# Expert-choice routing in a two-layer backbone: elementwise steps moved from GpSimd to VectorE, and the first expert's weight blocks split during the output projection

## The chip, the cores and the metric

The kernel runs on one core of a Trainium2 chip. A core has five engines, each with its own in-order instruction stream: TensorE (PE; its weight loads are shown as PEld), VectorE (DVE), ScalarE (ACT), GpSimd (POOL) and SyncE (SP), which here issues most of the DMA transfers. They wait for each other by semaphores. The metric is the device time of one execution in microseconds (us), the median of the runs.

## The reference, cut to what matters

One inference step of a backbone with two layers over 1024 latent tokens and 128 prompt tokens of width 1024. Layer 0 mixes the tokens with a recurrent unit (RG-LRU), layer 1 with a spatial gating unit (SGU); each is followed by an expert-choice mixture of experts (MoE) with 16 experts.

```python
def _ec_moe(x, router, w_gate, w_up, w_down):
    cap = EC_FACTOR * (bsz * t) // N_EXPERTS            # 128 of the 1024 tokens, 16 of the 128
    aff = jax.nn.softmax(xf @ router, axis=-1)
    g, idx = lax.top_k(aff.T, cap)                      # every expert chooses its tokens
    xs = xf[idx]
    hh = jax.nn.silu(einsum('ecd,edf->ecf', xs, w_gate)) * einsum('ecd,edf->ecf', xs, w_up)
    out = einsum('ecf,efd->ecd', hh, w_down) * g[..., None]
    y = jnp.zeros_like(xf).at[idx.reshape(-1)].add(out.reshape(-1, d))
...
for l in range(DEPTH):
    y = mixer(hn)                                       # ends with the output projection "@ w_out"
    x = x + g1 * y
    hn = _rmsnorm(x, norm2_g[l]) * (1 + s2) + sh2
    x = x + g2 * _ec_moe(hn, ...)
```

## The kernel before

The tokens are worked on in nine chunks of 128: chunks 0 to 7 are the latent tokens, chunk 8 is the prompt. Weights come from memory in fp32 and are split into two f16 parts, so that each fp32 product becomes three f16 matmuls (high by high, high by low, low by high): ScalarE rounds a block to its upper half (line L1583 in the expert loop, `whi`), VectorE subtracts that from the block for its lower half (L1589, `wlo`). A block has 128 columns of a 1024 by 1024 matrix. An expert has three such matrices, 24 blocks.

**Output projection.** The mixer's output is multiplied by `w_out` chunk by chunk, the last part of `lru_mixer` and `sgu_mixer`. Behind each chunk its residual and norm are computed (class `Post`: `residual`, `turn`, `logits`, `gather`), which gives the router's logits of that chunk. `turn` transposes the normalized rows on PE (hT, L350), `logits_mul` is L361, `gather_mul` L374 (`pz`). Inputs of the next chunks are fetched on SP's queue. The last chunk, 8, overlaps the routing.

**Routing** (class `Route`). The softmax over the experts ends at L386. Then the 128th largest affinity of each expert is found by bisection over its bits in 15 rounds (`rounds`). A round is a chain through two engines: VectorE forms three candidates (L425) and a mask of affinities over them (L427), PE counts by eight small matmuls with ones (L433), VectorE evaluates the counts (L434) and takes the largest (L435), and the next round starts from that. `finish` (from L444) compares with the found threshold and derives the slots of the tokens. The remaining work of chunk 8 is put between these steps by hand: `within[r]` (D in `lead`) holds functions that run between round r's mask and its counts, `after[r]` (R) those that run after its evaluation. `lead` places them relative to round v, which is 5 in layer 0 and 3 in layer 1: `take` multiplies y by the gate and adds it to x (on POOL, L315 and L316; in layer 0 for two halves of 512 columns, in layer 1 for one), then `squares`, `var`, `norm`, `turn(8)`, `halve` (chunk 8's rows as a rounded copy `xph` on ScalarE, L533, and the rest `xpl` on POOL, L534), the logits, the prompt's weights and their spreading.

**Start of the experts' weights.** Raw weights come in loads of 2 MB (L1574), each half a matrix, that is four blocks, into five buffers (`raw`). The five first loads are issued ahead of round 3. With `AHEAD = 3` the first three pairs of blocks are split before the expert loop begins: as many as fit (`route.v + r < 13`) during the rounds by `split_first` (two ScalarE passes, then the subtraction on POOL, L1602), the others after them.

**Expert loop** (`for n in range(NPAIR)`). An expert is twelve groups n of 48 matmuls (L1698) on two blocks: groups 0 to 3 with `w_gate`, 4 to 7 with `w_up`, 8 to 11 with `w_down`. The first 36 matmuls of a group take the first six of eight row slices of both blocks, the last 12 the other two. Groups 0 to 7 read the expert's tokens (`Sh`, `Sl`). Groups 4 to 7 give hidden blocks: t (VectorE, L1714), Hh (ScalarE, L1719, for the last one VectorE, L1721), Hl (VectorE, L1722). Groups 8 to 11 read these. Between the groups' matmuls the later blocks are split, in an order that the tables HIS and LOS give as counts for three places of a group (`ahead(n, 0)` and `ahead(n, 1)` between the group's two parts, `ahead(n, 2)` behind it). `whi` and `wlo` are rings of 12 buffers. At the end of layer 1 the final norm runs in the last expert's groups (class `Final`; its gains on POOL are L1816).

Of the kernel before, what the change touches and what calls it, by code (L numbers as in the profile page):

```python
# [43 lines left out]
def tile_trunk(  # L44
# [186 lines left out]
    def rows(ch):  # L231
        return slice(ch * P, (ch + 1) * P)
# [10 lines left out]
    class Post:  # L243
# [59 lines left out]
        def last(self, yps):  # L303


            l, xt, t = self.l, state["x8"], self.xnp
            g1 = self.g1 if self.apart else gate_row(l, 0, self.pool)
            ss = sm.tile([P, 2], F32, tag="ss2", name=f"pss{l}_8")
            s1, r, v, rr = (sm.tile([P, 1], F32, tag="last", name=f"last{l}_{i}", bufs=4) for i in range(4))
            cs = slice(0, 512), slice(512, 1024)  # L310

            def take():
                for n in sorted(yps):
                    A.activation(t[:, cs[n]], yps[n], AF.Copy, scale=1.0 / (UP * DOWN))
                    G.tensor_tensor(t[:, cs[n]], t[:, cs[n]], g1 if self.apart else g1[:, cs[n]], op=OP.mult)  # L315
                    G.tensor_tensor(xt[:, cs[n]], xt[:, cs[n]], t[:, cs[n]], op=OP.add)  # L316

            def squares():
                for n in sorted(yps):
                    A.activation(t[:, cs[n]], xt[:, cs[n]], AF.Square, accum_out=ss[:, n:n + 1])  # L320

            def var():
                V.tensor_add(s1, self.ss0[:, 8:9] if self.apart else ss[:, 0:1], ss[:, 1:2])
                V.tensor_scalar(v, s1, 1.0 / D, EPS, op0=OP.mult, op1=OP.add)
                G.tensor_tensor(r, v, half, op=OP.pow)

# [7 lines left out]
            return take, squares, var, norm  # L334

# [40 lines left out]
        def gather_keep(self, ch):  # L376
            V.tensor_copy(self.lg[:, ch], self.pz)

    def softmax(l, lg, af, ex):
# [9 lines left out]
    class Route:  # L389
# [93 lines left out]
        def inform(self, part):  # L483

            info, afs, t0 = self.info, self.af[:, 0:8], self.t0
            if part == 0:
                V.tensor_copy(info[:, :, :, 2], afs)
                V.tensor_copy(info[:, :, :, 0:2], tok_c[:, :, None, :].to_broadcast([P, 8, NE, 2]))
                V.tensor_tensor(t0, afs, info[:, :, :, 2], op=OP.subtract)
            else:  # L490
                V.tensor_copy(info[:, :, :, 3], t0)
                V.tensor_tensor(t0, t0, info[:, :, :, 3], op=OP.subtract)
                V.tensor_copy(info[:, :, :, 4], t0)

# [35 lines left out]
        def halve(self):  # L530
            xnp = self.post.xnp.rearrange("t (k p) -> t k p", p=P)
            self.xh, self.xl = (self.room(n, [P, KD, P], F32R) for n in ("xph", "xpl"))
            A.copy(self.xh, xnp)  # L533
            G.tensor_tensor(self.xl, xnp, self.xh, op=OP.subtract)  # L534

# [52 lines left out]
        def lead(self, y8, yps):  # L588


            post = self.post
            take, squares, var, norm = post.last(yps)
            for f in y8[:7]:
# [14 lines left out]
            v = self.v = s + 3  # L608
            R[s].append(take)
            R[v - 1].append(squares)  # L610
            D[v].append(var)
            D[v + 1].append(norm)
            R[v + 2].append(lambda: post.turn(8))
            D[v + 3].append(lambda: self.inform(0))
            R[v + 3].append(self.halve)
            D[v + 4].append(lambda: self.inform(1))
            R[v + 4].append(lambda: post.logits_mul(8))
            D[v + 5].append(lambda: post.logits_keep(8))
            R[v + 5].append(lambda: post.gather_mul(8))
            D[v + 6] += [lambda: post.gather_keep(8), self.weigh]  # L620
            D[v + 7].append(self.share)
            for q in range(4):
                R[v + 7 + q // 2].append(lambda q=q: self.spread(q))
# [6 lines left out]
    def lru_mixer(carry_of):  # L630
# [444 lines left out]
        def split_hg(ch):  # L1075
            hh = tmp("ae", f"hgh{ch}", 2, F16)[:, 0:9 * P].rearrange("p (h t) -> p h t", t=P)
            hl = tmp("hs", f"hgo{ch}", 2, F16)[:, 0:9 * P].rearrange("p (h t) -> p h t", t=P)
            split_up(hgs[ch], hh, hl, DOWN)
            return hh, hl
# [45 lines left out]
        def y_of(ch):  # L1125
            return [ps3.tile([P, 512], F32, tag="y", name=f"y0_{ch}_{n}", bufs=4) for n in range(2)]

        post.fetch(0)
        for ch in range(8):
            hl = nxt  # L1130
# [14 lines left out]
            else:  # L1145
# [14 lines left out]
                post.gather(ch - 1)  # L1160
            post.residual(ch, 1, yps[1])
        hl = nxt
        yps = y_of(8)
# [4 lines left out]
        route.settle(pool_of(ew, "l0x", side="right"))  # L1168
        return post, route, ew.close


    def sgu_mixer(carry_of):
# [72 lines left out]
        def fetch(ch):  # L1245
            if ch < 8:
                xs[ch] = kp.tile([P, D], F32, tag="pr", name=f"x1_{ch}", bufs=4)
                SP.dma_start(xs[ch], x_d[rows(ch), :])

        def norm(*chs):  # L1250
# [7 lines left out]
            for i, ch in enumerate(chs):  # L1258
                x = xs[ch]
                if ch == 8:  # L1260
                    xs[ch] = kp.tile([P, D], F32, tag="pr", name="x1_8", bufs=4)
                V.tensor_scalar_mul(xs[ch], x, r[:, i:i + 1])
# [49 lines left out]
        def load_spatial():  # L1312
            ws = state["ws"] = kp.tile([P, SGG, P], F32, tag="pr", name="ws", bufs=4)
            SP.dma_start(ws, sg_w_s[0].rearrange("g p q -> p g q"))
            SP.dma_start(bsr, sg_b_s[0])
# [173 lines left out]

        post = Post(1, pb, ps1, carry, alloc, apart=True)  # L1490
        post.xt[8] = state["x8"][:, 0:512]
        post.fetch_half(0)
        y, gates = {(0, 0): yps}, {}
        for c in range(1, 68):
# [22 lines left out]
            elif n == 0:  # L1517
# [30 lines left out]
        route.settle(pool_of(ew, "l1x", side="right"))  # L1548
        return post, route, ew.close


    def moe(l, post, route, carry, close):
        es = ExitStack()
# [12 lines left out]

        def load(m, eng=SP):

            if m >= 6 * NE or m == 5 and eng is SP:
# [4 lines left out]
            eng.dma_start(t, w[l, e].rearrange("(k p) f -> p k f", p=P)[:, :, 512 * half:512 * (half + 1)])  # L1574

# [4 lines left out]
        def split_hi(n, b):  # L1580
            if n < NPAIR:
                hi = wp.tile([P, KD, P], F16, tag="whi", name=f"whi{l}_{n}_{b}", bufs=12)
                A.activation(hi, block(n, b), AF.Copy, scale=UP)  # L1583
                ws[n, b] = [hi]

        def split_lo(n, b):
            if n < NPAIR:
                lo = wp.tile([P, KD, P], F16, tag="wlo", name=f"wlo{l}_{n}_{b}", bufs=12)
# [6 lines left out]
        def split_first(n, b):  # L1595

            up = mp.tile([P, KD, 144], F32, tag=("xg", "tmp")[b], name=f"wup{l}_{n}_{b}")[:, :, 0:P]
            A.activation(up, block(n, b), AF.Copy, scale=UP)
            hi = wp.tile([P, KD, P], F16, tag="whi", name=f"whi{l}_{n}_{b}", bufs=12)
            A.copy(hi, up)  # L1600
            lo = wp.tile([P, KD, P], F16, tag="wlo", name=f"wlo{l}_{n}_{b}", bufs=12)
            G.tensor_tensor(lo, up, hi, op=OP.subtract)  # L1602
            ws[n, b] = [hi, lo]
            if n % 2 == 1 and b == 1:
                raws.pop(n // 2)
                load(n // 2 + 5)

# [78 lines left out]


# [243 lines left out]
    for l, mixer in enumerate((lru_mixer, sgu_mixer)):  # L1931
# [6 lines left out]

        post, route, close = mixer(carry_of)
        moe(l, post, route, pools[l], close)  # L1940
        ec.close()
# [57 lines left out]
```

## Time and profile before

| | us |
|---|---|
| median of 3 runs | 2603.92 (2603.43 to 2604.54) |
| profiled execution, in all | 2600.83 |
| its span, first to last instruction | 2599.0 |
| busy: PE 94%, DVE 74%, ACT 63%, POOL 11% of the span | 2431.4, 1914.7, 1640.6, 293.2 |
| memory traffic over the span | 248 GB/s |

The profile is of one execution. Its times are in us from the start of the span, unless ns is written. A line such as L425 is a line of the kernel as printed above. In the timeline, a row is a start, a duration, the engine, line and operation, the tile written and the tile read with shapes and types, how many instructions the row joins (x8), and in brackets how long the engine had been idle before it and what released it. [...] The output projection of layer 0 lies in 400 to 520, its routing in 525 to 566, its expert loop from 581; in layer 1 the projection's second half lies in 1781 to 1889, the routing in 1888 to 1927, the expert loop from 1941.

### The profile page before, as it was taken

The numbers are of one execution on the slowest core, as the hardware profiler recorded it, in microseconds if no ns is written. First come the engines' busy times: TensorE is split into PE (matmuls) and PEld (weight loads), VectorE is DVE, ScalarE is ACT, GpSimd is POOL, SyncE is SP. The second block draws the span as 40 slices with busy tenths as digits, with TensorE's granted clock in tenths as the row PEclk, the third lists the DMA queues.
The fourth block names the chain that finished last, engine by engine and source line by source line (L and its number), as shares of the span: only waits on it lengthen the run. The fifth ranks groups of instructions, "written<-read, shape, count | busy, mean of one in ns | idle before, by whom it ended". The sixth has DMA issues, their size and how long they took to land. (4 is left out here: it accounts for less than half of the span.)

```text
span 2599.0 us, 60553 instructions
## 1 busy us (share of the span) xinstructions
PE 2431.4 (94%) x26054; PEld 1850.1 (71%) x26054; DVE 1914.7 (74%) x2771; ACT 1640.6 (63%) x2348; POOL 293.2 (11%) x324
## 2 busy tenths in 40 slices
PE   6999989959999999997999999999959999999995
PEld 4555554439999999997434455534549999999995
DVE  6888895479999989996622233445689999999997
ACT  5877883347877877785623333433357877777874
POOL 1011101120000000001201100100120000000003
PEclk9999999969999999998999999999969999999998
DMA  9466215359999999995544533455649999999994
GB/s 316 169 205 205 76 63 163 131 197 343 347 351 359 347 337 356 353 348 162 180 151 165 174 114 110 153 189 191 205 182 347 344 357 361 343 334 360 343 358 173
DMA packets 317755, 647.19 MB, mean 249 GB/s; under 512 B 15362, under 2 KB 52790, under 8 KB 317486
## 3 DMA queue, kind: packets, MB, share of 16 engines
q1 hardware_dynamic: 291792, 564.30, 61.0%
q0 software_dynamic: 21136, 74.67, 9.0%
q10 hardware_dynamic: 4558, 4.35, 0.5%
q8 instruction: 204, 3.34, 0.5%
q14 instruction: 65, 0.53, 0.1%
HBM read 576.59 MB, written 66.68 MB: 248 GB/s over the span
## 5 line engine op out<-in xcount | busy, mean ns | idle before, releaser
L1698 PEld LDWEIGHTS <-whi 128*128 128x128 f16 x12288 | 989.1, 98 | 30.6 <-issue 24.2
L1589 DVE SCALAR_TENSOR_TENSOR wlo<-raw,whi 128x1024 f16<-128x1024 f32 x759 | 894.3, 1219 | 20.7 <-ACT whi L1583 20.7
L1698 PE MATMUL mm<-Sh,whi 128*128 128x144 f16 x4096 | 774.8, 227 | 3.8 <-ACT tmp L1644 1.7
L1698 PE MATMUL mm<-Sl,whi 128*128 128x144 f16 x4096 | 774.7, 226 | 0.9 <-DVE Sl L1656 0.9
L1698 PE MATMUL mm<-Sh,wlo 128*128 128x144 f16 x4096 | 774.7, 227 | 0.0
L1583 ACT ACTIVATE whi<-raw 128x1024 f16<-128x1024 f32 x759 | 755.2, 1060 | 0.0
L1698 PEld LDWEIGHTS <-wlo 128*128 128x128 f16 x6144 | 602.4, 98 | 14.0 <-issue 14.0
L1698 PE MATMUL mm<-Hh,whi 128*128 128x144 f16 x2048 | 388.7, 226 | 19.0 <-DVE Hh L1721 14.8
L1698 PE MATMUL mm<-Hl,whi 128*128 128x144 f16 x2048 | 387.6, 226 | 8.6 <-DVE Hl L1722 8.6
L1698 PE MATMUL mm<-Hh,wlo 128*128 128x144 f16 x2048 | 387.6, 226 | 0.0
L1290 PE MATMUL uv<-sgw,h_hi 128*128 128x512 f16 x576 | 219.4, 381 | 0.0
L1291 PE MATMUL uv<-sgw,h_hi 128*128 128x512 f16 x576 | 219.3, 381 | 0.0
L1292 PE MATMUL uv<-sgw,h_lo 128*128 128x512 f16 x576 | 219.1, 380 | 0.0
L1296 ACT ACTIVATE uvo<-uv 128x512 f32<-128x512 f32 x72 | 42.9, 596 | 198.7 <-PE uv L1292 198.7
L1742 POOL DMA_INDIRECT x_d<-o,idx x31 | 58.0, 1870 | 959.6 <-ACT o L1741 897.7
L864 PE MATMUL pj<-hn_hi,wh 128*128 128x386 f16 x480 | 158.2, 330 | 1.9 <-ACT hn_hi L116 1.9
L865 PE MATMUL pj<-hn_lo,wh 128*128 128x386 f16 x480 | 157.8, 329 | 0.1
L866 PE MATMUL pj<-hn_hi,wl 128*128 128x386 f16 x480 | 157.9, 329 | 0.0
L1403 DVE SCALAR_TENSOR_TENSOR uvo<-sv,bs,uvo 128x256 f32<-128x256 f32 x72 | 31.5, 479 | 139.9 <-PE sv L1400 139.9
L1309 DVE TENSOR_TENSOR uvo<-uvo,gain 128x512 f32<-128x512 f32 x36 | 24.9, 691 | 133.8 <-ACT uv L1308 133.8
L1644 ACT ACTIVATE tmp<-xgT,modc,ns 128x128 f32<-128x128 f32 x248 | 90.2, 468 | 47.5 <-PE xgT L1631 38.8
L1709 ACT ACTIVATE sg<-mm 128x288 f32<-128x288 f32 x128 | 52.3, 409 | 94.5 <-PE mm L1698 94.3
(402 smaller groups left out, 3807.0 us busy)
## 6 DMA issues: line engine op xcount, KB each, us to landing
raw<-in_moe_w_gate_dram SPq DMA_DIRECT2D x64, 2048.0 KB
raw<-in_moe_w_up_dram SPq DMA_DIRECT2D x64, 2048.0 KB
raw<-in_moe_w_down_dram SPq DMA_DIRECT2D x62, 2048.0 KB
wm<-in_w_mod_dram SPq DMA_DIRECT2D x96, 512.0 KB
m<-mt_d SPq DMA_DIRECT2D x72, 256.0 KB
sgr<-in_sg_w_in_dram SPq DMA_DIRECT2D x32, 512.0 KB
win<-in_lru_w_in_dram SPq DMA_DIRECT2D x20, 512.0 KB
v_d<-uvo POOLq DMA_DIRECT2D x36, 256.0 KB, 2.5
```

The costliest lines, as they stand in the source:

```text
L864: PE.matmul(ps[:, i, 0:WP], wh[:, k], hi[k][:, cs], start=(k == 0), stop=False)
L865: PE.matmul(ps[:, i, 0:WP], wh[:, k], lo[k][:, cs], start=False, stop=False)
L866: PE.matmul(ps[:, i, 0:WP], wl[:, k], hi[k][:, cs], start=False, stop=(k == KD - 1))
L1290: PE.matmul(ps, hi[:, k, cs], th[:, k % 4], start=(k == 0), stop=False)
L1291: PE.matmul(ps, hi[:, k, cs], tl[:, k % 4], start=False, stop=False)
L1292: PE.matmul(ps, lo[:, k, cs], th[:, k % 4], start=False, stop=(k == KD - 1))
L1583: A.activation(hi, block(n, b), AF.Copy, scale=UP)
L1589: V.scalar_tensor_tensor(lo, block(n, b), UP, ws[n, b][0], op0=OP.mult, op1=OP.subtract)
L1644: A.activation(o, ps[h][:, k - 4 * h], AF.Identity, bias=sh2[:, 1, k:k + 1], scale=s2[:, 1, k:k + 1])
L1698: PE.matmul(ps[:, b, 0:144], w[:, k], x[:, k], start=(k == 0 and i == 0), stop=(k == KD - 1 and i == 2))
L1709: A.activation(sg[e][:, js], ps, AF.Silu, scale=1.0 / UP)
L1742: G.indirect_dma_start(out=x_d[0:NS, :], out_offset=bass.IndirectOffsetOnAxis(ap=idxs[:, e:e + 1], axis=0), in_=o, in_offset=None, compute ...
```

## The change

- `take` becomes `gate(n)` and `add(n)`, one VectorE instruction each on 512 columns, placed in `within`: half 1 in rounds v - 2 and v - 1, half 0, which only layer 0 has, in rounds 0 and 1.
- `inform` (VectorE, the affinities in three bf16 parts) is cut in four parts in four rounds.
- `halve` keeps the ScalarE copy; the subtraction goes to VectorE in two halves, `halve_rest(0)` in round v + 4 and `halve_rest(1)` in round v + 8.
- `split_first` and the load on ScalarE's queue are gone. A new class `First` loads the first eight blocks of expert 0's `w_gate` one by one (512 KB, SP's queue) and splits them on ScalarE and VectorE, one behind each of the chunks 0 to 7 of the output projection. The buffers for these loads are ones of the mixer. The rings `whi` and `wlo` keep 12 buffers and move to the pool that lives through both stages. `AHEAD` is 4, the 2 MB loads begin with number 2.
- In layer 0 `split_hg` takes one buffer for both halves; in layer 1 tiles tagged `pr` move to another pool.

```diff
@@ class Post, last
-            def take():
-                for n in sorted(yps):
-                    A.activation(t[:, cs[n]], yps[n], AF.Copy, scale=1.0 / (UP * DOWN))
-                    G.tensor_tensor(t[:, cs[n]], t[:, cs[n]], g1 if self.apart else g1[:, cs[n]], op=OP.mult)
-                    G.tensor_tensor(xt[:, cs[n]], xt[:, cs[n]], t[:, cs[n]], op=OP.add)
+            def gate(n):
+                V.scalar_tensor_tensor(t[:, cs[n]], yps[n], 1.0 / (UP * DOWN), g1 if self.apart else g1[:, cs[n]],
+                                       op0=OP.mult, op1=OP.mult)
+            def add(n):
+                V.tensor_add(xt[:, cs[n]], xt[:, cs[n]], t[:, cs[n]])
...
+    class First:
+        N = 8
+        def __init__(self, l, carry, room):
+            self.l, self.carry, self.room, self.raw, self.parts = l, carry, room, {}, []
+            self.src = moe_w_gate[l, 0].rearrange("(k p) f -> p k f", p=P)
+        def load(self, c):
+            if c < self.N:
+                self.raw[c] = self.room(f"first{self.l}_{c}").rearrange("p (k n) -> p k n", k=KD)
+                SP.dma_start(self.raw[c], self.src[:, :, rows(c)])
+        def split(self, c):
+            if c < self.N:
+                p = [self.carry.tile([P, KD, P], F16, tag=f"w{s}", name=f"w{s}{self.l}_f{c}", bufs=12) for s in ("hi", "lo")]
+                split_up(self.raw.pop(c), *p)
+                self.parts.append(p)
...
@@ class Route
         def halve(self):
-            xnp = self.post.xnp.rearrange("t (k p) -> t k p", p=P)
             self.xh, self.xl = (self.room(n, [P, KD, P], F32R) for n in ("xph", "xpl"))
-            A.copy(self.xh, xnp)
-            G.tensor_tensor(self.xl, xnp, self.xh, op=OP.subtract)
+            A.copy(self.xh, self.post.xnp.rearrange("t (k p) -> t k p", p=P))
+
+        def halve_rest(self, h):
+            ks = slice(4 * h, 4 * h + 4)
+            V.tensor_sub(self.xl[:, ks], self.post.xnp.rearrange("t (k p) -> t k p", p=P)[:, ks], self.xh[:, ks])
...
@@ lead
-            R[s].append(take)
+            for n in sorted(yps):
+                r = v - 2 if n else 0
+                D[r].append(lambda n=n: gate(n))
+                D[r + 1].append(lambda n=n: add(n))
+            D[v - 3].append(lambda: self.inform(0))
             R[v - 1].append(squares)
-            D[v].append(var)
+            D[v] += [var, lambda: self.inform(1)]
             D[v + 1].append(norm)
             R[v + 2].append(lambda: post.turn(8))
-            D[v + 3].append(lambda: self.inform(0))
+            D[v + 2].append(lambda: self.inform(2))
+            D[v + 3].append(lambda: self.inform(3))
             R[v + 3].append(self.halve)
-            D[v + 4].append(lambda: self.inform(1))
+            D[v + 4].append(lambda: self.halve_rest(0))
...
+            D[v + 8].append(lambda: self.halve_rest(1))
...
@@ lru_mixer, output projection
+        firsts = First(0, carry, lambda name: tmp("hs", name, 2)[:, 0:D])
         post.fetch(0)
+        for i in range(2):
+            firsts.load(i)
         for ch in range(8):
...
             post.residual(ch, 1, yps[1])
+            firsts.split(ch)
+            firsts.load(ch + 2)
...
@@ sgu_mixer, output projection
+        firsts = First(1, carry, lambda name: wp.tile([P, D], F32, tag="wr", name=name, bufs=4))
...
                 if ch == 8 and q == 3:
                     post.fetch(0)
+                    for i in range(3):
+                        firsts.load(i)
             else:
+                if q == 3:
+                    firsts.split(ch)
+                    firsts.load(ch + 3)
...
@@ moe
-                hi = wp.tile([P, KD, P], F16, tag="whi", name=f"whi{l}_{n}_{b}", bufs=12)
+                hi = carry.tile([P, KD, P], F16, tag="whi", name=f"whi{l}_{n}_{b}", bufs=12)
...
-        for m in range(5):
+        AHEAD = 4
+        for c, p in enumerate(firsts.parts):
+            ws[divmod(c, 2)] = p
+        for m in range(2, 7):
             load(m)
-        AHEAD = 3
-        first = [(n, b) for n in range(AHEAD) for b in range(2)]
-        for r in (1, 3, 4, 6, 9, 10):
-            if route.v + r < 13:
-                route.after[route.v + r].append(lambda nb=first.pop(0): split_first(*nb))
...
-        load(5, A)
...
-        for n, b in first:
-            split_hi(n, b)
-            split_lo(n, b)
         split_hi(AHEAD, 0)
```

## Rows read from the trace of the kernel before

**Rows 1.** Windows view: stretch, length, busy PE PEld DVE ACT POOL (instructions), PEclk, DMA, GB/s.
```profile
475.00:500.00 25.00, 25.00 (x153) 12.61 (x152) 9.56 (x20) 10.07 (x24) 2.22 (x4) 1.00 0.39 129
...
540.00:560.00 20.00, 6.99 (x84) 5.84 (x84) 17.72 (x44) 13.19 (x20) 8.74 (x4) 0.50 0.67 261
...
707.29:746.10 38.81, 38.27 (x603) 37.95 (x601) 35.66 (x49) 30.73 (x44) 3.20 (x2) 1.00 0.99 353
...
1880.00:1900.00 20.00, 11.58 (x108) 6.44 (x107) 14.44 (x45) 6.29 (x12) 4.18 (x6) 0.80 1.01 377
```

**Rows 2.** VectorE's timeline, routing of layer 0: start us, us, instruction, [idle <-releaser].
```profile
524.86 1.39 DVE L386 TENSOR_TENSOR af<-ex,mx 128x128 f32<-128x128 f32 x1
...
560.17 2.08 DVE L425 TENSOR_TENSOR cand<-cand,bits 128x48 int32<-128x48 int32 x1
...
566.03 0.29 DVE L444 TENSOR_TENSOR ge<-af,cand 128x128 bf16<-128x128 f32 x1
```

**Rows 3.** GpSimd's timeline, same stretch.
```profile
560.06 2.12 POOL L1602 TENSOR_TENSOR wlo<-wup,whi 128x1024 f16<-128x1024 f32 x1 [5.76 <-ACT whi L1600]
```

**Rows 4.** VectorE's timeline, routing of layer 1.
```profile
1887.78 0.29 DVE L386 TENSOR_TENSOR af<-ex,mx 128x128 f32<-128x128 f32 x1
...
1888.18 0.21 DVE L425 TENSOR_TENSOR cand<-cand,bits 128x48 int32<-128x48 int32 x1
...
1889.43 0.21 DVE L434 SCALAR_TENSOR_TENSOR cand<-cnt,cand 128x48 f32<-128x48 f32 x1 [0.45 <-PE cnt L433]
...
1889.96 0.21 DVE L425 TENSOR_TENSOR cand<-cand,bits 128x48 int32<-128x48 int32 x1
...
1927.27 0.29 DVE L444 TENSOR_TENSOR ge<-af,cand 128x128 bf16<-128x128 f32 x1
```

**Rows 5.** VectorE's and ScalarE's timelines, rounds 7 and 8 of layer 0.
```profile
541.26 0.21 DVE L425 TENSOR_TENSOR cand<-cand,bits 128x48 int32<-128x48 int32 x1
...
543.17 0.21 DVE L425 TENSOR_TENSOR cand<-cand,bits 128x48 int32<-128x48 int32 x1
...
543.78 2.90 ACT L350 ACTIVATE hT<-ptr,modc,ns 128x128 f32<-128x128 f32 x8
...
546.54 1.08 ACT L533 CAST rxph<-xnp 128x1024 fp32r<-128x1024 f32 x1
```

**Rows 6.** TensorE's timeline, logits of chunk 8, layer 0.
```profile
552.60 1.08 PE L361 MATMUL pl<-hT,rt 128*32 128x128 f32 x16 [4.43 <-DVE cand L434]
```

**Rows 7.** PE's, ACT's and DVE's timelines, groups 4 to 8 of an expert, layer 0.
```profile
713.24 3.89 ACT L1583 ACTIVATE whi<-raw 128x1024 f16<-128x1024 f32 x4
...
715.43 0.23 PE L1698 MATMUL mm<-Sl,whi 128*128 128x144 f16 x1
...
717.34 0.43 ACT L1719 CAST Hh<-t 128x288 f16<-128x288 f32 x1 [0.22 <-DVE t L1714]
...
717.81 0.46 DVE L1722 TENSOR_TENSOR Hl<-t,Hh 128x288 f16<-128x288 f32 x1 [0.50 <-ACT Hh L1719]
...
728.49 0.22 PE L1698 MATMUL mm<-Hh,whi 128*128 128x144 f16 x1 [0.27 <-DVE Hh L1721]
```

**Rows 8.** PE's and POOL's timelines, last experts of both layers.
```profile
1197.82 0.22 PE L1698 MATMUL mm<-Hh,whi 128*128 128x144 f16 x1 [1.08 <-DVE Hh L1721]
...
2554.94 6.00 POOL L1816 TENSOR_TENSOR fin<-fin,gain 128x1024 f32<-128x1024 f32 x2 [9.42 <-ACT fin L1809]
...
2561.16 0.28 PE L1698 MATMUL mm<-Hh,whi 128*128 128x144 f16 x1 [4.91 <-DVE Hh L1721]
...
2563.85 1.05 POOL L105 TENSOR_TENSOR rsrf<-rsvf,half 128x4 f32<-128x4 f32 x1 [2.91 <-DVE rsvf L103]
```

**Rows 9.** Page, section 5: operation, count | busy us, mean ns | idle before, releaser.
```profile
L1589 DVE SCALAR_TENSOR_TENSOR wlo<-raw,whi 128x1024 f16<-128x1024 f32 x759 | 894.3, 1219 | 20.7 <-ACT whi L1583 20.7
...
L1583 ACT ACTIVATE whi<-raw 128x1024 f16<-128x1024 f32 x759 | 755.2, 1060 | 0.0
```

**Rows 10.** TensorE's timeline, end of the output projection, layer 1.
```profile
1876.29 0.40 PE L374 MATMUL pz<-sel,ls 128*128 128x16 f32 x2 [0.49 <-DVE ls L366]
```

More of the change, by code (lines that the diff above doesn't have):

```diff
@@ L332, in norm @@
                 self.xn[8] = self.xnp
-            return take, squares, var, norm
+            return gate, add, squares, var, norm
         def turn(self, ch):
@@ L488, in inform @@
                 V.tensor_copy(info[:, :, :, 0:2], tok_c[:, :, None, :].to_broadcast([P, 8, NE, 2]))
+            elif part == 1:
                 V.tensor_tensor(t0, afs, info[:, :, :, 2], op=OP.subtract)
-            else:
+            elif part == 2:
                 V.tensor_copy(info[:, :, :, 3], t0)
                 V.tensor_tensor(t0, t0, info[:, :, :, 3], op=OP.subtract)
+            else:
                 V.tensor_copy(info[:, :, :, 4], t0)
@@ L591, in lead @@
             post = self.post
-            take, squares, var, norm = post.last(yps)
+            gate, add, squares, var, norm = post.last(yps)
             for f in y8[:7]:
@@ L1075, in split_hg @@
         def split_hg(ch):
-            hh = tmp("ae", f"hgh{ch}", 2, F16)[:, 0:9 * P].rearrange("p (h t) -> p h t", t=P)
-            hl = tmp("hs", f"hgo{ch}", 2, F16)[:, 0:9 * P].rearrange("p (h t) -> p h t", t=P)
+            t = tmp("ae", f"hgs{ch}", 2, F16)
+            hh, hl = (t[:, a:a + 9 * P].rearrange("p (h t) -> p h t", t=P) for a in (0, 9 * P))
             split_up(hgs[ch], hh, hl, DOWN)
@@ L1168, in lru_mixer @@
         route.settle(pool_of(ew, "l0x", side="right"))
-        return post, route, ew.close
+        return post, route, firsts, ew.close
     def sgu_mixer(carry_of):
@@ L1246, in fetch @@
             if ch < 8:
-                xs[ch] = kp.tile([P, D], F32, tag="pr", name=f"x1_{ch}", bufs=4)
+                xs[ch] = hp.tile([P, D], F32, tag="pr", name=f"x1_{ch}", bufs=4)
                 SP.dma_start(xs[ch], x_d[rows(ch), :])
@@ L1260, in norm @@
                 if ch == 8:
-                    xs[ch] = kp.tile([P, D], F32, tag="pr", name="x1_8", bufs=4)
+                    xs[ch] = hp.tile([P, D], F32, tag="pr", name="x1_8", bufs=4)
                 V.tensor_scalar_mul(xs[ch], x, r[:, i:i + 1])
@@ L1312, in load_spatial @@
         def load_spatial():
-            ws = state["ws"] = kp.tile([P, SGG, P], F32, tag="pr", name="ws", bufs=4)
+            ws = state["ws"] = hp.tile([P, SGG, P], F32, tag="pr", name="ws", bufs=4)
             SP.dma_start(ws, sg_w_s[0].rearrange("g p q -> p g q"))
@@ L1548, in sgu_mixer, with moe @@
         route.settle(pool_of(ew, "l1x", side="right"))
-        return post, route, ew.close
-    def moe(l, post, route, carry, close):
+        return post, route, firsts, ew.close
+    def moe(l, post, route, firsts, carry, close):
         es = ExitStack()
@@ L1565, in moe, with load @@
         NPAIR = 12 * NE
-        def load(m, eng=SP):
-            if m >= 6 * NE or m == 5 and eng is SP:
+        def load(m):
+            if m >= 6 * NE:
                 return
@@ L1573, in load @@
             w = (moe_w_gate, moe_w_up, moe_w_down)[which]
-            eng.dma_start(t, w[l, e].rearrange("(k p) f -> p k f", p=P)[:, :, 512 * half:512 * (half + 1)])
+            SP.dma_start(t, w[l, e].rearrange("(k p) f -> p k f", p=P)[:, :, 512 * half:512 * (half + 1)])
         def block(n, b):
@@ L1587, in split_lo @@
             if n < NPAIR:
-                lo = wp.tile([P, KD, P], F16, tag="wlo", name=f"wlo{l}_{n}_{b}", bufs=12)
+                lo = carry.tile([P, KD, P], F16, tag="wlo", name=f"wlo{l}_{n}_{b}", bufs=12)
                 V.scalar_tensor_tensor(lo, block(n, b), UP, ws[n, b][0], op0=OP.mult, op1=OP.subtract)
@@ L1593, in split_lo @@
                     load(n // 2 + 5)
[L1595 to L1606, printed above, removed]
         def slots_a(e):
@@ L1937, in carry_of @@
             return pools[l]
-        post, route, close = mixer(carry_of)
-        moe(l, post, route, pools[l], close)
+        post, route, firsts, close = mixer(carry_of)
+        moe(l, post, route, firsts, pools[l], close)
         ec.close()
```

## The prediction

> **What bounds the kernel now.** I read the busy time by stretch first, to see which engine fills each stage [rows 1]; the columns are the length, then the busy time of TensorE (PE), its weight loads, VectorE (DVE), ScalarE (ACT) and GpSimd (POOL), then TensorE's granted clock, DMA share and rate. Three stages touch the change. In the output projection PE is busy 25.00 of 25 us while DVE has 9.56 and ACT 10.07. In routing (540 to 560) PE has 6.99 of 20 at the lower level of its clock (0.50), and DVE 17.72: a serial stage, a DVE step, a PE count, a DVE step. In the expert loop, over one expert of 38.81 us, PE has 38.27. Then the timeline of DVE in routing [rows 2]: from the softmax's last step at 524.86 to the first comparison after round 14 at 566.03 layer 0 takes 41.17 us. The step L425 takes 2.08 us at 560.17; the same step takes 0.21 us at 1888.18 [rows 4]. POOL [rows 3] explains it: its subtraction L1602 runs from 560.06 to 562.18, and DVE's step ends at 562.25. DVE's stretched steps end with a POOL tensor operation, eight in layer 0 and six in layer 1. Last the waits in the expert loop: PE stops once an expert, for the last hidden block [rows 7].
>
> **Routing.** I rebuild a stage from rounds that nothing stretches. From the softmax step to round 0 is 0.40 us, a round at the full clock 1.78 [rows 4], at the lower clock 1.91 [rows 5]. Each new piece on DVE (gate, add, inform's parts, halves of the subtraction) stands between the mask and the counts' evaluation, where DVE waits for PE anyway. That wait is 0.45 us [rows 4]. A piece of 512 columns is half of a DVE pass over 1024, of 1.22 [rows 9]: 0.61. Steps in a row overlap by some 0.1 (four ACT passes of 1.06 take 3.89 [rows 7, 9]), so I charge 0.61 - 0.45 - 0.10 = 0.06 at the full clock, bounds 0 and 0.16, and 0 at the lower, where a round is 0.13 longer. If that cover were gone, two gates, two adds and two halves in layer 0 and one, one and two in layer 1 would cost ten times 0.61 = 6.1 us. Layer 0: six rounds of 1.84 and nine of 1.91 are 28.2. To this come the rounds in which PE has other work ahead of the count (transposes, the logits, the spreading): 1.3 together, an estimate from the nearest row, the logits' 1.08 us that start only after an evaluation [rows 6], bounds 0 and 2.5.
>
> The change adds one wait that I can place. VectorE now takes the first half of the subtraction in program order, two rounds after the turn of chunk 8, and it needs ACT's rounded copy xph. In before hT starts 2.52 us after round 7 (541.26, 543.78) and takes 2.90; xph follows at 546.54 for 1.08 [rows 5]. Freed of the weight work hT can start some 0.2 us sooner, no more, since the transposes gate it; so xph is done 6.2 us after round 7 begins. VectorE stands before it after two rounds (1.91 and 2.1) and 0.7 us, at 4.7. It waits 1.5 us; queued behind it are the count's evaluation, thus the next round, and PE's logits. Bounds 0 and 2.5. Layer 0: 0.40 + 28.2 + 1.3 + 1.5 = 31.4, against 41.2: **9.7 less**. Layer 1 runs 39.49 from 1887.78 to 1927.27 [rows 4]; after, three rounds of 1.83 and twelve of 1.91 give 28.4, with 0.40, 1.3 and 1.5 it is 31.6: **7.9 less**. ScalarE's weight splits (two passes a block) leave routing too; they were off the path there, as were POOL's products themselves but for what they held up.
>
> **Output projection.** Sixteen blocks are split here, each one ACT pass of 1.06 us, one DVE pass of 1.22 [rows 9] and one 512 KB load on SP's queue, put behind that chunk's hidden rows and x fetch. A layer's eight take 18 us over both engines, spread over eight chunks; there DVE and ACT are idle over half the time [rows 1], and the loads are asked a chunk or more ahead. SP is in order: a load that waits for its buffer holds the next chunk's fetches, but the buffer is free once the split before is done, at the end of its chunk. I cost this at nothing in layer 0. In layer 1 the last block's lower half stands in front of the copy that pz waits for, where PE already stops 0.49 us for it [rows 10]: 0.4, bounds 0 and 1.2. Routing and projection together: 9.7 + 7.9 - 0.4 = **17.2 us less**.
>
> **Expert loop.** The lead goes from three pairs of blocks to four; the rings whi and wlo keep 12 buffers. Three pairs plus what the schedule runs ahead never met the ring's end. With four, the block that ScalarE rounds at the end of group 4 of each expert (group: 48 matmuls on two blocks) takes the buffer of group 4's own first block, whose last reader is its 41st matmul. In [rows 7] this 41st matmul starts at 715.43. ScalarE now does its four blocks without a gap from 713.24, 0.95 apart, so the third starts at 715.13, and Hh follows at 717.34, as soon as t is done. After, the third starts at 715.69 (0.26 behind that matmul's start, PE's pipe), the fourth at 716.64, Hh at 717.59: **0.25 later**. DVE stands at Hl waiting for Hh (0.50 idle) and has no gap from there to the last Hh, for which PE waits at 728.49: the delay reaches PE whole. In groups 5 to 7 the same wait falls into ACT's idle time before Hh. Thirty experts times 0.25 is 7.5 us more; bounds 0, and 0.69 each (20.7) if the buffer only comes free with the group's last matmul (seven of 38.27 / 603 = 0.063 us later [rows 1]).
>
> In the last expert of a layer two blocks fewer are left to split, so DVE reaches the last Hh with the matmuls: layer 0's stop of 1.08 goes [rows 8]. In layer 1 PE's stop of 4.91 there has another part, POOL's gains of 6.00 us from 2554.94, which move by 0.5 at most; POOL's next step at 2563.85 can follow them at 2561.5, 2.3 earlier. Together -3.4, bounds 0 and -5. The start of the loop I leave: its first weights are ready in before too, and the lower clock there costs the same. Loop: 7.5 - 3.4 = **4.1 more**.
>
> The sum is -17.2 + 4.1 = **-13.1 us**. The profiled execution has a span of 2599.0 and 2600.8 in all, 3.1 below the median of 2603.92; I take the difference over: 2590.8.
>
> **Rivals.** *Ring without a price*: if ScalarE stands differently against PE, the buffer is free in time; then -17.2 - 3.4 = -20.6, 2583.3. For it: 0.25 is small against an expert of 38.8 us; against: four blocks without a gap. *Ring at its full price*: 0.69 an expert, -17.2 + 20.7 - 3.4 = 0.1, 2604.0. Against it: the releases have been by block where I could see them. *Pieces not hidden*: DVE's pieces lengthen their rounds by their whole length, 6.1: -7.0, 2596.9. That is also how the change would fail to do what it says, stalls exchanged for work of the same chain. For it: the fit is close, 0.06 us over at the full clock. *Slower*: the splitting in the output projection comes onto PE's path. If both passes of each of the 16 blocks do (1.06 + 1.22), it is 36.5 us: +23.4, 2627.3; it decides from 13.1 / 16 = 0.82 us a block. For it: ACT and DVE also carry normalization, and both are in order; against: half of either is idle. *Transfers as the bound*: the loop moves 353 GB/s at a share of 0.99 [rows 1]. If that were the limit, the loop's end would be set by its loads: two loads of 2.1 MB fewer a layer, 5.9 us each, less 5 us because the first load of the loop comes later, on top of routing's 8.6: 15.3 a layer, -30.6, 2573.3. Against it: ScalarE, which reads the loads first, stops 0.0 us ahead of its passes [rows 9], and in layer 1's routing 377 GB/s ran [rows 1]. [...]
>
> **How the numbers follow.** Forecast 0.55, ring free 0.15, ring at full price 0.10, pieces not hidden 0.08, slower projection 0.08, transfers 0.04. Against 0.2% (5.2 us), which a measurement can tell from no change, faster are the forecast, the free ring, the unhidden pieces and the transfers: 0.82; same the full ring price: 0.10; slower 0.08. The range leaves out the slower projection and the transfers and takes in the ring's and the xph wait's bounds: 2580 to 2604.
>
> **What would show it.** No DVE step of over 0.8 us in the rounds but one that waits for xph; layer 0's stage at 31.4 and layer 1's at 31.6; no DVE pass longer than its kind. In the loop: Hh of group 4 about 0.25 later against the group's start, PE's stop before the last Hh 0.5 instead of 0.27, an expert 39.06 instead of 38.81. PE at 25 of 25 in the projection; if not, the fourth rival. I am wrong if the expert period grows by over 0.6, or if rounds exceed 2 us where PE has no other work.

## The result, and the profile of the changed kernel

The changed kernel takes 2587.38 us (median of 4 runs, 2585.74 to 2591.89) against 2603.68 for the kernel before on the same chip (2599.24 to 2604.54): the medians are 16.3 us apart. The ratio worked out from the runs is 0.9945 with a 95% interval of 0.9933 to 0.9957, which is 14.3 us less, between 11.2 and 17.4. The forecast was 2590.8, 13.1 less. The two profiled executions differ by 14.2 us (spans of 2599.0 and 2584.8). By stages of these two, in us:

| stage | before | after | measured | forecast |
|---|---|---|---|---|
| routing, layer 0 | 41.17 | 31.44 | -9.73 | -9.7 |
| routing, layer 1 | 39.49 | 31.45 | -8.04 | -7.9 |
| one expert of the middle | 38.81 | 39.07 | +0.26 | +0.25 |
| expert loop, layer 0 | 626.93 | 628.67 | +1.74 | +2.7 |
| expert loop and what follows, layer 1 | 658.22 | 660.87 | +2.65 | +1.4 |
| start to layer 0's routing | 524.86 | 523.63 | -1.23 | 0 |
| loop of layer 0 to layer 1's routing | 679.84 | 681.09 | +1.25 | +0.4 |
| end of the rounds to the loops, both | 28.50 | 27.69 | -0.81 | 0 |

The "forecast" loops take 15 experts at 0.25 and the terms for the last experts. The -1.23 is no part of the change: TensorE's steps stand apart by that much at 370 us, where no step was changed, and still at 525. This stretch differs by more between the other profiles: over all profiles of this study layer 0's routing begins between 523.3 and 527.0 us. So the stages below are compared by their own lengths.

The windows view of the changed kernel, columns as in [rows 1]: output projection, routing of layer 0 and of layer 1, one expert:

```profile
475.00:500.00 25.00, 25.00 (x154) 12.55 (x153) 11.31 (x21) 11.65 (x27) 1.98 (x4) 1.00 0.65 194
...
523.63:555.07 31.44, 17.35 (x181) 12.91 (x180) 26.03 (x89) 9.54 (x27) 0.56 (x1) 0.67 0.89 335
...
1878.98:1910.43 31.45, 14.75 (x169) 11.89 (x168) 26.05 (x88) 11.55 (x31) 0.57 (x1) 0.66 0.88 334
...
685.02:724.09 39.07, 38.29 (x603) 37.97 (x601) 35.68 (x49) 31.08 (x44) 3.12 (x2) 1.00 0.99 350
```

In the projection PE is busy for 25.00 of 25 us as in [rows 1], with DVE at 11.31 instead of 9.56 and ACT at 11.65 instead of 10.07: the splits lie beside the matmuls. In routing POOL is busy for 0.56 us; 16.91 before. DVE has 26.03 of 31.44, 34.64 of 41.17 before: with more steps to do it is busy 8.6 us less, so at least that much of its "work" was waiting.

VectorE's timeline of two early rounds and of the ones around xph, layer 0:

```profile
524.75 0.68 DVE L313 SCALAR_TENSOR_TENSOR xnp<-y,g_None 128x512 f32<-128x512 f32 x1
525.35 0.20 DVE L455 SCALAR_TENSOR_TENSOR cand<-cnt,cand 128x48 f32<-128x48 f32 x1
...
525.87 0.21 DVE L446 TENSOR_TENSOR cand<-cand,bits 128x48 int32<-128x48 int32 x1
...
541.24 0.56 DVE L448 TENSOR_TENSOR mask<-af,cand 128x384 bf16<-128x384 f32 x1
543.17 0.69 DVE L559 TENSOR_TENSOR rxpl<-xnp,rxph 128x512 fp32r<-128x512 f32 x1 [1.38 <-ACT rxph L555]
543.78 0.20 DVE L455 SCALAR_TENSOR_TENSOR cand<-cnt,cand 128x48 f32<-128x48 f32 x1
...
546.18 0.21 DVE L455 SCALAR_TENSOR_TENSOR cand<-cnt,cand 128x48 f32<-128x48 f32 x1 [0.57 <-PE cnt L454]
```

The gate's piece of 0.68 fits ahead of the evaluation at 525.35; this round takes 1.84 us. The one long wait is that of the first half of the subtraction, 1.38 us for xph. L446 (L425 before) takes 0.21 in every round of both layers; [rows 2] has it at 2.08.

In the expert loop, ScalarE's timeline for group 4 of the fourth expert, VectorE's and TensorE's for what waits for it, the expert of [rows 7]:

```profile
702.04 2.00 ACT L1626 ACTIVATE whi<-raw 128x1024 f16<-128x1024 f32 x2
704.49 2.01 ACT L1626 ACTIVATE whi<-raw 128x1024 f16<-128x1024 f32 x2 [0.46 <-PE mm L1722]
706.41 0.42 ACT L1743 CAST Hh<-t 128x288 f16<-128x288 f32 x1
...
704.23 0.23 PE L1722 MATMUL mm<-Sl,whi 128*128 128x144 f16 x1
...
706.86 0.46 DVE L1746 TENSOR_TENSOR Hl<-t,Hh 128x288 f16<-128x288 f32 x1 [0.74 <-ACT Hh L1743]
...
717.54 0.22 PE L1722 MATMUL mm<-Hh,whi 128*128 128x144 f16 x1 [0.51 <-DVE Hh L1745]
```

Four passes without a gap in [rows 7] are now two and two, with 0.46 us between them that a matmul ends: the wait for the buffer. The third block starts 0.26 behind the 41st matmul of the group (704.23), as the forecast had it. Hl waits 0.74 for Hh (0.50 before), PE 0.51 for the last Hh (0.27 before). Section 5 of the page shows the waits for TensorE as 49.8 us, where [rows 9] has no idle time; group 5's (0.73 us ahead of its first pass at 707.55) are in it too, and there ScalarE still waits for t afterwards, ahead of Hh:

```profile
L1626 ACT ACTIVATE whi<-raw 128x1024 f16<-128x1024 f32 x752 | 756.0, 1060 | 53.3 <-PE mm L1722 49.8
```

### The profile page after: what moved, and what is told of

Read it like the earlier page. It is cut to its first block, busy times and chain, and to the rows that moved or that the text cites. A ratio compares the mean times of both kernels' runs of the same rounds, so it can differ in the third digit from the quotient of the medians.

```text
span 2584.8 us, 60548 instructions
## 1 busy us (share of the span) xinstructions
PE 2432.3 (94%) x26054; PEld 1850.6 (72%) x26054; DVE 1909.0 (74%) x2790; ACT 1641.5 (64%) x2336; POOL 257.6 (10%) x307
## 5 line engine op out<-in xcount | busy, mean ns | idle before, releaser
L1722 PEld LDWEIGHTS <-whi 128*128 128x128 f16 x12032 | 966.8, 98 | 28.0 <-issue 22.2
L1626 ACT ACTIVATE whi<-raw 128x1024 f16<-128x1024 f32 x752 | 756.0, 1060 | 53.3 <-PE mm L1722 49.8
L1722 PE MATMUL mm<-Sh,whi 128*128 128x144 f16 x3968 | 747.6, 226 | 0.8 <-DVE t L1738 0.8
L1722 PE MATMUL mm<-Sh,wlo 128*128 128x144 f16 x3968 | 747.6, 226 | 0.0
L1722 PE MATMUL mm<-Sl,whi 128*128 128x144 f16 x3968 | 747.6, 226 | 0.0
L1722 PEld LDWEIGHTS <-wlo 128*128 128x128 f16 x6016 | 589.2, 98 | 13.9 <-issue 13.7
L1327 PEld LDWEIGHTS <-h_hi 128*128 128x128 f16 x576 | 56.5, 98 | 69.4 <-issue 10.1
```

The lines of the kernel that those rows point to most:

```text
L1327: PE.matmul(ps, hi[:, k, cs], th[:, k % 4], start=(k == 0), stop=False)
L1722: PE.matmul(ps[:, b, 0:144], w[:, k], x[:, k], start=(k == 0 and i == 0), stop=(k == KD - 1 and i == 2))
```

## The experiments

Theory: VectorE's steps were held by GpSimd's, and the change removes that; the loop pays for it because the lead of eight blocks meets the end of the ring of 12. Rivals: only one of the two kinds of GpSimd work mattered; the longer lead costs by itself or by its loads; GpSimd's end would have done as well. The kernels e1 to e4 take the change apart, e5 to e10 go after its remaining waits. Stage lengths are each from one profile:

| kernel | routing 0 | routing 1 | one expert | last expert, layer 0 / 1 | median (runs) |
|---|---|---|---|---|---|
| before | 41.17 | 39.49 | 38.81 | 38.49 / 46.33 | 2603.68 (4) |
| changed | 31.44 | 31.45 | 39.07 | 36.82 / 45.49 | 2587.38 (4) |
| e1_ring13 | 31.46 | 31.53 | 38.82 | 36.81 / 43.91 | 2578.17 (4) |
| e2_lead3 | 31.50 | 31.35 | 38.82 | 38.49 / 46.40 | 2587.06 (1) |
| e3_poolprod | 33.54 | 31.55 | 39.06 | 36.82 / 45.27 | 2590.08 (1) |
| e4_poolsplit | 35.45 | 35.62 | 38.81 | 38.49 / 46.33 | 2593.34 (1) |
| e5_poolsub | 30.50 | 30.41 | 39.06 | 36.82 / 45.31 | 2584.50 (1) |
| e6_xphlater | 30.04 | 30.06 | 39.06 | 36.82 / 44.43 | 2583.53 (1) |
| e7_gains | 31.24 | 31.30 | 39.06 | 36.82 / 36.81 | 2576.38 (1) |
| e8_together | 29.70 | 30.16 | 38.81 | 36.81 / 36.81 | 2569.13 (4) |
| e9_gains_order | 31.33 | 31.62 | 39.06 | 36.82 / 36.82 | 2583.11 (1) |
| e10_together_order | 29.73 | 30.17 | 38.81 | 36.81 / 36.81 | 2569.86 (4) |

The kernel before has medians of 2599.67 to 2603.68 on the chips of these runs. e1's four runs lie 9.1 us apart, so a single run decides nothing of a few us; the argument goes by the stages.

**e1_ring13**: the ring of upper halves with 13 buffers.

```diff
@@ class First, split
-                p = [self.carry.tile([P, KD, P], F16, tag=f"w{s}", name=f"w{s}{self.l}_f{c}", bufs=12) for s in ("hi", "lo")]
+                p = [self.carry.tile([P, KD, P], F16, tag=f"w{s}", name=f"w{s}{self.l}_f{c}", bufs=b) for s, b in (("hi", 13), ("lo", 12))]
...
@@ moe, split_hi
-                hi = carry.tile([P, KD, P], F16, tag="whi", name=f"whi{l}_{n}_{b}", bufs=12)
+                hi = carry.tile([P, KD, P], F16, tag="whi", name=f"whi{l}_{n}_{b}", bufs=13)
```

> The changed kernel with 13 buffers instead of 12 in the ring of upper halves (whi) alone; nothing else. Theory (the ring's end costs 0.26 us an expert): the third block that ScalarE rounds in group 4 takes a buffer that is long free, the fourth takes the one that the 41st matmul releases, which is early enough. Period of an expert 38.81 instead of 39.07, 30 x 0.26 = 7.8 us less, about 2579.6 where the changed kernel has 2587.4. Rival (the longer lead itself, its loads or the order of work cost the 0.26): the period stays 39.07 and the time 2587.

Measured: 2578.17 (2574.90 to 2583.96), ratio to before 0.9907 (0.9888 to 0.9926), 9.2 less than the changed kernel's median, which was taken on another chip. One expert is 38.82, and ScalarE's four passes are without a gap again, Hh 0.22 behind them as in [rows 7]:

```profile
704.55 3.89 ACT L1626 ACTIVATE whi<-raw 128x1024 f16<-128x1024 f32 x4
708.66 0.43 ACT L1743 CAST Hh<-t 128x288 f16<-128x288 f32 x1 [0.22 <-DVE t L1738]
```

The loads and the lead are the changed kernel's, so the 0.26 us are the ring's end.

**e2_lead3**: six blocks ahead instead of eight.

```diff
-        N = 8
+        N = 6
...
-        AHEAD = 4
+        AHEAD = 3
...
-        for m in range(2, 7):
+        for m in range(1, 6):
```

> The changed kernel with six blocks split ahead instead of eight (N = 6, AHEAD = 3, 2 MB loads from number 1), ring of 12 as it is. Theory (the lead empties the last experts and overfills the ring): period back at 38.81, and the stop ahead of the last expert's group 8 comes back in layer 0 (last expert 38.5 instead of 36.8 us); net about -7.8 + 1.7 + 1 = -5 against the changed kernel. Rival (the ring has no part in it): period 39.07; the last expert as in the changed kernel.

Measured: 2587.06 in its one run; expert 38.82, last experts 38.49 and 46.40 as before the change. Both halves of the theory stand: the short lead takes the ring's wait away and brings the last expert's stop back. The total did not fall by 5 in this run. In its profile the loops and what follows are 4.1 us shorter than the changed kernel's (627.21 + 635.04 + 23.22 against 628.67 + 637.49 + 23.38), and the stretches ahead of both routings 3.5 longer; there its edit only leaves out the last two of eight splits. The stretches ahead of the routings move by as much between other profiles.

**e3_poolprod** and **e4_poolsplit** part the two kinds of GpSimd work. e3 keeps the early splits and puts the products and the subtraction back on GpSimd; e4 is the kernel before with the changed routing and its own splits on GpSimd in the rounds.

```diff
 e3, from the changed kernel
+            def take():
+                for n in sorted(yps):
+                    A.activation(t[:, cs[n]], yps[n], AF.Copy, scale=1.0 / (UP * DOWN))
+                    G.tensor_tensor(t[:, cs[n]], t[:, cs[n]], g1 if self.apart else g1[:, cs[n]], op=OP.mult)
+                    G.tensor_tensor(xt[:, cs[n]], xt[:, cs[n]], t[:, cs[n]], op=OP.add)
...
+            G.tensor_tensor(self.xl, xnp, self.xh, op=OP.subtract)
```

> The changed kernel with the gate and add products and the subtraction of chunk 8 on GpSimd as in the kernel before; the early splits stay. Theory (any GpSimd tensor operation holds VectorE up until its end): two gates, two adds and one subtraction in layer 0 stretch VectorE steps again; layer 0's stage 31.4 + 3.5 = 35, layer 1's 31.4 + 2 = 33.4, loop as in the changed kernel. Rival (only the splits' subtractions hurt, being right behind one another): both stages stay at 31.4 or fall by 1.4, since VectorE no longer waits for the rounded copy xph.

> The kernel before with the routing's elementwise steps of the changed kernel (gate, add, inform, subtraction in pieces on VectorE), its weight splits left in the routing on GpSimd, AHEAD 3. Theory: the four subtractions of 2.13 us in the rounds still stretch VectorE steps, about 1.8 us each: stages 31.4 + 7 = 38.4 in both layers, expert period 38.81, in all about 2600. Rival (the products carried the loss): stages near 31.4 and 2586.

Measured: e3 33.54 and 31.55 where 35 and 33.4 were expected, e4 35.45 and 35.62 where 38.4 were. Each kind alone costs less than expected, and neither rival holds in layer 0: the splits alone cost 4.0 us (35.45 - 31.44), the products with the subtraction 2.1. In layer 0 of e4 the four splits stretch a mask to 2.39 us (0.56 by itself) and three steps that form candidates to 0.90, 0.71 and 2.08 (0.21 by themselves), while VectorE's wait for xph is 0.89 instead of 1.38. Against the kernel before, e4 saves 5.72 and 3.87, e3 7.63 and 7.94, the whole change 9.73 and 8.04, less than their sum. Both kernels also have `inform` in four parts, and in the kernel before three of layer 0's eight stretched steps were `inform`'s; what placing these anew saved is thus in both figures, and no kernel has it alone. How much of the shortfall is this, and how much that in before one VectorE step waited where another would have, is not shown.

What I had wrong in e3 is the subtraction. In layer 1, e3 is as fast as the changed kernel: its products cost 1.27 in their round (3.12 against 1.85), the subtraction gives 0.94 back (round v + 4 takes 1.91 instead of 3.31, round v + 6 takes 2.45 instead of 1.99), other rounds the rest. GpSimd's and VectorE's timelines of it in e3:

```profile
547.66 2.73 POOL L556 TENSOR_TENSOR rxpl<-xnp,rxph 128x1024 fp32r<-128x1024 f32 x1 [8.30 <-ACT rxph L555]
```

```profile
547.61 0.56 DVE L447 TENSOR_TENSOR mask<-af,cand 128x384 bf16<-128x384 f32 x1
548.38 0.29 DVE L366 COPY ls<-pl 128x128 f32<-128x128 f32 x1 [0.21 <-PE pl L361]
549.24 0.21 DVE L454 SCALAR_TENSOR_TENSOR cand<-cnt,cand 128x48 f32<-128x48 f32 x1 [0.57 <-PE cnt L453]
549.48 0.26 DVE L455 TENSOR_REDUCE cand<-cand 128x16 f32<-128x64 f32 x1
549.77 0.67 DVE L445 TENSOR_TENSOR cand<-cand,bits 128x48 int32<-128x48 int32 x1
```

The subtraction runs from 547.66 to 550.39. In that time VectorE does the copy from `pl`, the evaluation from `cnt` and the reduction at their usual lengths; only L445 is held, by 0.46, until GpSimd has ended. This GpSimd step of 2.73 us cost VectorE 0.46, not its own length: the step that it held came up 0.62 before its end.

**e5_poolsub** and **e6_xphlater** go after the 1.38 us that VectorE waits for xph.

```diff
 e5
+            G.tensor_tensor(self.xl, xnp, self.xh, op=OP.subtract)
...
-            D[v + 4].append(lambda: self.halve_rest(0))
-            D[v + 8].append(lambda: self.halve_rest(1))
 e6
-            D[v + 4].append(lambda: self.halve_rest(0))
-            D[v + 5].append(lambda: post.logits_keep(8))
+            D[v + 5] += [lambda: post.logits_keep(8), lambda: self.halve_rest(0)]
```

> The changed kernel with chunk 8's subtraction back on GpSimd as one operation; gate and add stay on VectorE. Theory (VectorE's wait for the rounded copy xph costs more than GpSimd's hold of one VectorE step): round v + 4 falls from 3.31 to 1.91, round v + 6 rises by 0.46 as in the kernel with GpSimd's products; a stage of 30.5 us instead of 31.4 in both layers. Rival (any step on GpSimd costs what it lasts, 2.1): 32.1 or more.

> The changed kernel with the first half of the subtraction one round later, behind the copy of the logits. Theory (xph is then done, nothing waits for it): round v + 4 falls from 3.31 to 1.91, the next grows by 0.1 or 0.2 from 2.41; a stage of 30.2 us, 2.4 less over both layers. Rival (the logits or their copy are what the rounds wait for, and the wait moves along): 31.4 as before.

Measured: e5 30.50 and 30.41, e6 30.04 and 30.06. In e5 round v + 4 takes 1.91 and round v + 6 2.47 (3.31 and 1.99 in the changed kernel); in e6 they take 1.91 and 1.99, and round v + 5 2.41 as ever: the piece costs nothing there. Of the change, moving this subtraction to VectorE where it was put lost 0.9 to 1.0 us a layer against leaving it on GpSimd.

VectorE in e6; the subtraction has no wait in front of it, and the evaluation none behind it:

```profile
545.17 0.29 DVE L367 COPY ls<-pl 128x128 f32<-128x128 f32 x1 [0.21 <-PE pl L362]
545.38 0.68 DVE L559 TENSOR_TENSOR rxpl<-xnp,rxph 128x512 fp32r<-128x512 f32 x1
546.03 0.21 DVE L455 SCALAR_TENSOR_TENSOR cand<-cnt,cand 128x48 f32<-128x48 f32 x1
```

**e7_gains**, **e9_gains_order**: the end of layer 1, where GpSimd's gains were part of the sum [rows 8]. The gains of chunks 0 to 5 (`gains`, on GpSimd) and the multiplication by the norm's factor (`scale`, on VectorE or ScalarE) become one VectorE instruction a chunk (`norm`). In e7 chunks 4 and 5 are written after the last expert's rows, so that e7 leaves the last expert out of those rows; e9 has them in order.

```diff
 e7 and e9, one of the lines
-                st[11] = [lambda: self.squares(6, 7), lambda: self.gains(3), lambda: self.scale(V, 1)]
+                st[11] = [lambda: self.squares(6, 7), lambda: self.norm(1), lambda: self.norm(2)]
...
 e9 alone
-                self.norm(7)
+                for ch in (7, 4, 5):
+                    self.norm(ch)
```

> The changed kernel with the final norm's gains of chunks 0 to 5 not on GpSimd but in VectorE's last multiplication (1.28 us a chunk instead of 0.74), chunks 3 to 5 leave ScalarE. Theory (in layer 1's last expert GpSimd's six gains hold VectorE's small steps and with them TensorE): the last expert takes 37.5 instead of 45.5, the steps behind it 1 more than 23.4; 7 us less in all. Rival (the stretched steps are covered by other waits, the norm's chain above all): the last expert stays over 43 and the time within 2 us.

> As e7_gains, with chunks 4 and 5 multiplied and written ahead of the last expert's rows (in e7_gains and e8_together they were written after them, so that those rows of the output kept a state without the last expert). Theory: two multiplications of 1.28 us now stand in front of the last rows' norm on VectorE, some 2.6 us, of which part is hidden by TensorE's prompt products: last expert 36.8, the steps behind it 1 to 3 longer than in e7_gains, 2577 to 2579. Rival (all hidden): 2576.

Measured: last expert 36.82 in both, as in layer 0, and 24.3 and 24.2 us behind it (23.4 in the changed kernel): 7.8 us less in the stage, by the theory. Of e9's expectation the rival holds: the two multiplications are hidden. Its one run of 2583.11 is above e7's 2576.38, though its two routings, loops and end are only 0.4 longer; the stretches ahead of the routings and between rounds and loop, in which the two do not differ, make the rest.

The changed kernel's last groups show how GpSimd held VectorE there:

```profile
2548.37 9.27 POOL L1840 TENSOR_TENSOR fin<-fin,gain 128x1024 f32<-128x1024 f32 x4
```

```profile
2542.37 2.57 DVE L1746 TENSOR_TENSOR Hl<-t,Hh 128x288 f16<-128x288 f32 x1
...
2548.42 2.33 DVE L111 TENSOR_TENSOR rstf<-rsrf 128x4 f32<-128x4 f32 x1 [1.23 <-POOL rsrf L105]
2550.78 2.27 DVE L112 SCALAR_TENSOR_TENSOR rstf<-rstf,rsvf 128x4 f32<-128x4 f32 x1
2553.09 2.26 DVE L113 SCALAR_TENSOR_TENSOR frstd<-rstf,rsrf 128x4 f32<-128x4 f32 x1
2555.27 0.41 DVE L1752 TENSOR_TENSOR oT<-mm,g 128x256 f32<-128x256 f32 x1
...
2555.84 0.30 PE L1722 MATMUL mm<-Hh,whi 128*128 128x144 f16 x1 [4.00 <-DVE pt L1753]
```

Three steps on 128x4 elements take 2.3 us each, as long as one gain each; in e9, without the gains, each takes 0.16:

```profile
2551.57 0.16 DVE L112 SCALAR_TENSOR_TENSOR rstf<-rstf,rsvf 128x4 f32<-128x4 f32 x1
```

Behind the three in the changed kernel stand L1752 and L1753, which take TensorE's results out of its output buffers, and PE is idle for 4.00 us until the second has ended. The windows view of these stretches shows what that does to PE, and the last one the whole last expert in e9:

```profile
2546.00:2550.00 4.00, 4.00 (x68) 4.00 (x66) 2.77 (x4) 3.90 (x7) 3.83 (x3) 1.00 0.01 4
2550.00:2556.00 6.00, 2.00 (x32) 1.82 (x30) 5.93 (x6) 0.47 (x2) 6.00 (x4) 0.90 0.00 0
2556.00:2562.00 6.00, 6.00 (x52) 6.00 (x51) 3.47 (x5) 0.00 (x0) 1.63 (x1) 0.53 0.42 169
```

```profile
2520.19:2557.01 36.82, 36.82 (x586) 36.81 (x584) 28.84 (x41) 26.27 (x38) 4.47 (x3) 1.00 0.52 181
```

**e8_together**, **e10_together_order**: ring, later half and gains in one kernel; e8 with the order of e7, and so without the last expert in the same rows, e10 with the order of e9.

> The changed kernel with the ring of 13, the first half of the subtraction a round later and the final gains on VectorE. Theory: the three add up, -7.8 - 2.4 - 7 = -17.2 against the changed kernel, 2570. Rival (they meet the same wait, or the clock falls at another place): less than 12 in all.

> As e8_together with the order of e9_gains_order. Theory: expert period 38.81, stages of 30.1, last expert 36.8; e8_together's 2569 plus what e9_gains_order loses, 2570 to 2572, some 16 less than the changed kernel. Rival (the new order puts the norm on the end's path in full): 2573 or more.

Measured: e8 2569.13, ratio 0.9889 (0.9873 to 0.9906); e10 2569.86 (2568.85 to 2571.96) against 2602.80 for the kernel before on that chip, ratio 0.9877 (0.9860 to 0.9893). The three add up, e10 to 17.5 less than the changed kernel's median on another chip, and no new wait takes their place: expert 38.81, last experts 36.81 in both layers, routing 29.73 and 30.17. e10 beats both kernels.

## Why the prediction was right

**Routing.** Rebuilding a stage from rounds that nothing stretches gave 31.4 and 31.6; 31.44 and 31.45 were measured. The pieces cost what was charged: 1.84 and 1.85 against 1.79 in a round without. The wait for xph was 1.38 where I had 1.5. The rounds in which PE has other work took 1.4 more than plain rounds in layer 0, where 1.3 was charged from a single row with bounds of 0 and 2.5; these two estimates erred by 0.1 each, in opposite directions, and such closeness is in part luck. The rival of pieces that are not hidden falls by the row at 525.35, that of slower projection by PE's 25.00 of 25. What the sum did not ask is whether this subtraction had to move; e5 and e6 show 0.9 and 1.4 us a layer for that.

**Why a held step.** The rows of e3 show that L445, whose two inputs lie both in SBUF, is held (0.67 instead of 0.21), while the steps there that read PSUM (0.29 and 0.21) or reduce one input (0.26) are not. GpSimd's subtraction takes 2.73 there, of which 2.22 lie behind the end of the mask L447 at 548.17; a split's subtraction of the same size takes 2.12 [rows 3]. I read this as the mask, there first, holding GpSimd; it is one pair of steps. Two inputs are not the whole condition: in the kernel before a copy and a cast of `inform`, with one input each in SBUF, are stretched too, while GpSimd splits blocks.

```profile
544.02 2.27 DVE L488 COPY info<-tok_c 128x256 bf16<-128x256 bf16 x1
...
550.27 2.15 DVE L493 CAST info<-t 128x128 bf16<-128x128 f32 x1
...
543.96 2.13 POOL L1602 TENSOR_TENSOR wlo<-wup,whi 128x1024 f16<-128x1024 f32 x1 [4.79 <-ACT whi L1600]
...
550.04 4.27 POOL L1602 TENSOR_TENSOR wlo<-wup,whi 128x1024 f16<-128x1024 f32 x2
```

In the changed kernel the same two take 0.39 and 0.34. What the two engines wait for in each other is not shown; the rows give only which steps were held, and by how much.

**Projection.** Nothing in layer 0, by its row above. In layer 1 PE waits 0.93 us ahead of pz, 0.49 in [rows 10]: 0.44 where I had 0.4.

```profile
1867.49 0.40 PE L375 MATMUL pz<-sel,ls 128*128 128x16 f32 x2 [0.93 <-DVE ls L367]
```

**Loop.** The mechanism and its 0.26 us were right, by e1 and e2. The count was off: 30 experts were charged, 26 pay. In each layer the first expert has other waits (its time rose by 0.07 and 0.51, and it lies between 39.2 and 41.5 over all profiles), the last has fewer splits, and the tenth, which also does the first half of the prompt's products, takes 42.66 before and 42.67 after. The full ring price (0.69 an expert) is refuted, and the transfers do not set the 39.07: in e1 the expert is shorter at 0.99 of the DMA engines' time, with 356 GB/s in place of 350.

**Last experts.** This is the term whose mechanism did not hold: -3.4 charged, -2.9 in the two profiles. In layer 0 it is -1.67 against -1.08 (the stops of both Hh and Hl went), and so it is in every kernel with eight blocks ahead. In layer 1 it is -0.84 - 0.35 = -1.2 against -2.3, but this number moves: the last expert and what follows take 70.06 us before, 68.87 in the changed kernel, and 67.7 to 68.3 in e3, e5 and e6, which change nothing there (66.9 in e1). So the size of -2.3 is not refuted. What failed is the step "POOL's next step at 2563.85 can follow them at 2561.5, 2.3 earlier", as if the end moved with it. GpSimd's rsrf did start earlier, at 2547.33 or, with the 13.0 us by which this expert began earlier, 3.5 us sooner; group 8 took 4.84 instead of 9.09. But behind it VectorE's three steps wait for the next gains as before, groups 10 and 11 take 7.16 and 5.61 instead of 5.72 and 2.95, and PE, idle for 4.0 of 6 us, comes back at a granted clock of 0.53; in the kernel before the same groups ran at 1.00. e9 takes the gains away, and PE is then busy 36.82 of 36.82 at 1.00.

By the two profiles the terms of the sum come to 12.9 less (-9.73 - 8.04 + 1.74 + 2.65, and 0.44 for pz), where 13.1 was forecast: the routing terms are right each by itself, while the errors in the loops, +1.2 in layer 1 and -0.9 in layer 0, nearly cancel, which is luck. From 12.9 to the 14.2 of the spans there are the stretches of the table that were charged with nothing. The largest of them, ahead of layer 0's routing, is no part of the change; of the 0.8 between rounds and loops, from which the change takes the last splits, it is not shown how much is its doing. The 16.3 of the medians lies within the interval of 11.2 to 17.4.

## What to carry to other kernels

Durations far above their kind that ended with another engine's operation were waits here: L425's 2.08 us at 560.17 ended 0.07 behind GpSimd's subtraction [rows 2, 3], and in the changed kernel the step takes 0.21 in all 30 rounds. Rebuilt from the undisturbed pieces, such a stage came within 0.15 us of the measured one here, with two terms that were off by 0.1 each way. Before moving work between two engines, ask which steps it can hold at that moment (0.46 us by the 2.73 of e3), and whether the new engine will wait, with the steps queued behind, for an input that the old one could wait for at no cost (1.38 us for xph on VectorE here). When a lead grows, count the ring's buffers: one buffer more was worth 0.26 us in each of 26 experts here, 6.8 us beside the 14 to 16 of the whole change.

## What the runs showed that I had not expected

A GpSimd operation of 2.7 us beside the rounds cost VectorE only 0.46 us in e3, while one of 2.12 cost it 1.87 in [rows 2, 3]; beside the first ran a copy, an evaluation and a reduction at their usual 0.29, 0.21 and 0.26, and the step that it held came up late. And a stop of PE at the very end was paid twice: after 4.0 idle us of 6 the granted clock fell to 0.53, and 48 matmuls of the last group took 5.61 us instead of 2.95. The kernel before paid so in another place: after its stop of 4.91 [rows 8] the clock was 0.66 from 2561 to 2566, and the 48 matmuls of group 9 took 3.69 us instead of 3.00.
